# One decoder step on one core: a fixed order of products up to the MLP, more 48-product sequences, a second norm by fp32r products, and a shared last multiplication

## The chip, the cores and the metric

The kernel runs on 1 core of one Trainium2 chip. A core has a matrix engine (TensorE, in the profile PE for products and PEld for weight loads), three engines for elementwise work (VectorE or DVE, ScalarE or ACT, GpSimd or POOL), SyncE (SP) that issues transfers, and 16 DMA engines. The metric is the device time of one execution in microseconds (us). The kernel before has a median of 1088.29 us over three runs (1088.22 to 1089.59).

## The reference

One layer of a hybrid decoder is computed for 256 prompt positions and 8 x 4 sample positions, T = 288 columns in all, in float32:

```
h = rmsnorm(x, norm1_g);  proj = h @ w_in + b_in          # 2048 -> 3072
a, gate, z = proj split at 1024, 2048
u = a * sigmoid(gate)                                     # gated group
c = silu(layernorm(depthwise_conv31(history ++ u)))       # 1024 channels
d = windowed means of (history ++ z) - z                  # windows 2, 4, 8, 16, one per group of 256
p = (d_g @ pool_w[g] for 4 groups) * pool_scale           # 1024 channels
x = x + concat(c, p) @ w_out                              # 2048 -> 2048
h2 = rmsnorm(x, norm2_g)
x = x + square(relu(h2 @ w_ff1)) @ w_ff2                  # 2048 -> 8192 -> 2048
y = rmsnorm(x, norm_f)
```

The last 30 values of u and 15 of z are returned as new states. The columns of the norms are independent, so a row scale (1/rms) can be applied after a projection; the kernel does that.

## The kernel before

Channels lie on the 128 partitions, the 288 positions along the free axis, so x is 16 tiles of 128x288. Each float32 operand is split into a high part in fp32r (hi) and the remainder (lo), and a product is three fp32r products: hi x hi, hi x lo, lo x hi. `gemm` (line 291) issues them: two output tiles (m) at a time, input tiles (k) in pairs, six products per pair and m. An input tile's hi and lo lie in one four-row tile, and `classes` in `gemm` reorders the first products of a call by the row that they stream, as a string of 0 and 1 tells; `TURN` (line 70) is such a string for 48 products. It is used in four calls: c2, the third group of each half of w_out, and the third group of ff1.

Weights come from HBM in blocks of 8 input tiles, 256 columns wide (`load`, line 159), each in two halves of 128x1024; `split` (line 281) makes hi by ScalarE (L265) and lo by VectorE (V, L270), GpSimd (G, L273) or an accumulating DMA (D), as the table `WAYS` says for each stage. There are six buffers for raw halves and five for split ones. `ready` holds the weights made ahead for the next call; a call takes one entry and makes the next at its end.

The work goes through these stages, in the order of the program:
- a first pass over x with four output banks (c0 and c1 of the gated group) during the loads; the sum of squares for the first norm (`squares`, `first_sums`, `first_rows`) is reduced by small products on TensorE (L230), a root, and a spreading product (L250);
- `SEQUENCE` (line 45): c is a gated convolution pair (`conv_pair`: the 31 taps run as low-priority steps on VectorE, L434), p the projection of one pooling group (`pool_group`: GpSimd sums of line 466, VectorE's last split of d into `dx` at L478), P the pooling product `pool_products` that reads dx;
- w_out over the pooling half (`mixp`), with the products of the layernorm (`ln_mean`, `ln_sums`, `ln_rows`) in between, then over the convolution half (`mixc`);
- four rounds of ff1 (8 groups of 256 columns, 96 products each) and ff2. The second norm's sum of squares `ss2` is added up by GpSimd (L604); after the first ff1 group it goes through `rsqrt_rows` and scales each group's output;
- the last norm: small products, a root, spreading products, and a multiplication of the 16 tiles by VectorE in six pieces (L652), each followed by its store from SP's queue (L653).

A planner lays out each engine's instructions: by the rank in which the program traced them, among those whose inputs are ready in its own timeline. `later()` puts work at a low rank. `tc.issue_after(ins)` keeps what it covers behind `ins` on the same engine. In the kernel before, TensorE's order is therefore the planner's except in a few places; it put P1 into c7 and P0 into the first w_out group.

Of the kernel before, what the change touches and what calls it, by code (L numbers as in the profile page):

```python
# [16 lines left out]
P = 128  # L17
# [27 lines left out]
SEQUENCE = [(_s[0], int(_s[1])) for _s in "c0 c1 c2 c3 c4 p3 c5 p2 P3 c6 p1 P2 p0 P1 c7 P0".split()]  # L45
# [41 lines left out]
def trunk_kernel(ctx: ExitStack, tc: tile.TileContext, io):  # L87
# [133 lines left out]
    def rsqrt_sums(parts, scale, after=None, busy=(0, 0)):  # L221
# [5 lines left out]
        idle = cvp.tile([P, 512], F32, name=nm("idle"), tag="cv") if sum(busy) else None  # L227
        for n, t in enumerate(parts):
            for j in range(3):
                last = nc.tensor.matmul(pt[:TB, j : j + 1], t[:, j * TB : (j + 1) * TB], ones[:, 0:1], start=n + j == 0, stop=n == len(parts) - 1 and j == 2)  # L230
            with tc.issue_after(last.ins):
                for j in range(busy[n] if n < 2 else 0):
                    nc.tensor.matmul(idle[:, 0:P], ones, ones, start=True, stop=True)  # L233
# [12 lines left out]
    def spread(sums):  # L246

        s, pr, _ = sums
        for j in range(3):
            last = nc.tensor.matmul(pr[:, j * TB : (j + 1) * TB], s[:, j : j + 1].to_broadcast([TB, P]), ident, start=j == 0, stop=j == 2)  # L250
        return pr, last

    def rsqrt_rows(*args):
        return spread(rsqrt_sums(*args))[0]

# [34 lines left out]

    def gemm(banks, rhs, m_outer=False, between={}, classes=""):
# [3 lines left out]
        gets = ready.pop()  # L295
        step = 2 if len(banks) == 2 else 1
        pairs = [(k, m) for k in range(0, n, step) for m in range(len(banks))]
        if m_outer:
            pairs.sort(key=lambda km: km[1])
        if step == 2:  # L300
            parts = ((0, 0, 0), (1, 0, 0), (0, 1, 0), (1, 1, 0), (1, 0, 1), (0, 0, 1))
        else:
            parts = ((0, 0, 0), (0, 0, 1), (0, 1, 0))
        todo = [(k + d, m, w, x) for k, m in pairs for d, w, x in parts]
# [5 lines left out]
        ahead = None  # L310
        for j, (k, m, w, x) in enumerate(todo):
            if j % (len(banks) * len(parts)) == 0:
                ahead = between[k]() if k in between else None
            with tc.issue_after(ahead.ins) if ahead is not None else nullcontext():
                last = nc.tensor.matmul(banks[m][:, :T], gets[k // 8](k % 8, m)[w], rhs[k][x], start=j == ends[m][0], stop=j == ends[m][1])  # L315
# [167 lines left out]
    def pool_products(g):  # L483

        bk = ms("pp")
        gemm(each(bk), halves(dd[g]))
        for m, (mh, ml) in enumerate(halves(dd[g])):
# [3 lines left out]
            mixp[i] = (mh, ml)  # L491

# [15 lines left out]
    with tc.issue_after(gemm(pair0 + pair1, hx, between={15: first_sums})):  # L508
        third = conv_products(2, between={2: first_rows}, classes="01" * 18 + TURN)
# [3 lines left out]
    conv_pair(2, third)  # L513
    for kind, i in SEQUENCE[3:]:
        if kind == "c":
            conv_pair(i, conv_products(i))
        elif kind == "p":
            pool_group(i)
        else:
# [8 lines left out]
    def ln_mean():  # L528
        norm["mean"] = ms("pmean")[:, 0, :T]
        nc.tensor.matmul(norm["mean"], ones, sum_c[:, 0, :], start=True, stop=False)  # L530
        return nc.tensor.matmul(norm["mean"], ones, cs[-1][:, 1, :], start=False, stop=True)
# [20 lines left out]
    behind = nullcontext()  # L552
    for g in range(8):
        bk = bank2()
        with behind:
# [156 lines left out]
```

## Time and profile before

| | |
|---|---|
| median of 3 runs | 1088.29 us |
| profiled execution | 1087.97 us |
| its span, first to last instruction | 1086.2 us |
| mean granted TensorE clock | 0.997 |
| TensorE's products | 8206, busy 1073.7 us |
| VectorE / ScalarE / GpSimd busy | 634.0 / 477.9 / 182.7 us |
| read from HBM / written | 185.16 / 4.28 MB |

The profile shows one execution. A row of a timeline gives start, length, engine, line, operation, output and inputs, and how many instructions were merged, in brackets the idle time before and what ended it. A row of a stretch gives busy time and, in brackets, the instructions touched for each engine, then the granted clock, the share of the DMA engines and GB/s. Products are pipelined: one lasts some 0.29 us while the next starts after 0.13, so starts and not lengths show the pace.

### The profile page before, as it was taken

What the parts mean: (1) busy time and instruction counts of PE and PEld (TensorE: products, weight loads), DVE (VectorE), ACT (ScalarE), POOL (GpSimd) and SP (SyncE); (2) the same over time, 40 slices, a digit from 0 to 9 for tenths busy, and PEclk for the clock granted to TensorE, in tenths of its full rate; (3) what the DMA queues carried; (4) which work ended last, traced back from release to release, by engine and by line L of the source; (5) the groups of instructions that cost most, each with busy time, mean ns of one, the idle gap of its engine ahead of it and who ended that gap; (6) DMA issues with size and microseconds to landing.
All of it is one profiled execution on the core that took longest, in us unless ns stands there. A gap on an engine that the chain in (4) does not pass through costs nothing.

```text
span 1086.2 us, 19609 instructions
## 1 busy us (share of the span) xinstructions
PE 1073.7 (99%) x8206; PEld 1071.4 (99%) x8206; DVE 634.0 (58%) x813; ACT 477.9 (44%) x583; POOL 182.7 (17%) x212
## 2 busy tenths in 40 slices
PE   9999999999999999999999999999999999999996
PEld 8999999999999999999999999999999999999996
DVE  7899999678555444445454444545544445554553
ACT  8654445475544433334443333444433334444441
POOL 0888989613000000000000000000000000000000
PEclk9999999999999999999999999999999999999998
DMA  9896467545455555555555555555555555555522
GB/s 333 281 269 177 136 178 245 183 153 178 159 171 169 164 172 174 166 167 173 167 167 172 172 165 168 175 167 165 174 169 165 172 173 165 167 174 166 168 76 88
DMA packets 58120, 190.71 MB, mean 176 GB/s; under 512 B 6192, under 2 KB 11312, under 8 KB 58032
## 3 DMA queue, kind: packets, MB, share of 16 engines
q1 hardware_dynamic: 56480, 185.27, 52.2%
q0 software_dynamic: 1008, 3.67, 1.9%
q8 instruction: 64, 1.05, 0.4%
q10 hardware_dynamic: 544, 0.52, 0.1%
q14 instruction: 24, 0.20, 0.0%
HBM read 185.16 MB, written 4.28 MB: 174 GB/s over the span
## 4 chain that ended last, share of the span: by engine, by line
PE 96%; DVE 1%; ACT 1%; DMA 1%; issue 1%; POOL 0%; DVEq 0%
PE ac L315 95%; DMA wr<-in_w 1%; PE pp L315 0%; DVE xT L652 0%; ACT whi L265 0%; DVE wlo L270 0%; POOL wlo L273 0%; PE idle L233 0%; ACT n L567 0%; PE pt L250 0%; PE pt L230 0%; DVE z_all L391 0%; ACT z_all L389 0%; ACT hx L340 0%; DVE n L564 0%
## 5 line engine op out<-in xcount | busy, mean ns | idle before, releaser
L265 ACT CAST whi<-wr 128x1024 fp32r<-128x1024 f32 (+1 forms) x341 | 356.6, 1046 | 558.4 <-PE ac L315 540.4
L270 DVE TENSOR_TENSOR wlo<-wr,whi 128x1024 fp32r<-128x1024 f32 (+1 forms) x295 | 362.9, 1231 | 350.3 <-ACT whi L265 350.3
L315 PE MATMUL ac<-ax,whi 128*128 128x288 f32 x2048 | 351.5, 292 | 0.0
L315 PE MATMUL ac<-fx,whi 128*128 128x288 f32 x2048 | 350.1, 292 | 0.0
L315 PEld LDWEIGHTS ac<-ax,whi 128*128 128x128 f32 x2048 | 296.2, 187 | 0.0
L315 PEld LDWEIGHTS ac<-fx,whi 128*128 128x128 f32 x2048 | 295.6, 187 | 0.0
L315 PE MATMUL ac<-ax,wlo 128*128 128x288 f32 x1024 | 217.4, 292 | 0.0
L315 PE MATMUL ac<-fx,wlo 128*128 128x288 f32 x1024 | 216.3, 292 | 0.0
L315 PEld LDWEIGHTS ac<-ax,wlo 128*128 128x128 f32 x1024 | 162.7, 187 | 0.0
L315 PEld LDWEIGHTS ac<-fx,wlo 128*128 128x128 f32 x1024 | 162.2, 187 | 0.0
L315 PE MATMUL ac<-hx,whi 128*128 128x288 f32 x768 | 136.3, 295 | 0.6 <-DVE hx L338 0.6
L315 PEld LDWEIGHTS ac<-hx,whi 128*128 128x128 f32 x768 | 113.8, 188 | 1.0 <-ACT whi L265 0.8
L273 POOL TENSOR_TENSOR wlo<-wr,whi 128x512 fp32r<-128x512 f32 x78 | 105.9, 1411 | 32.7 <-ACT whi L265 30.4
L434 DVE SCALAR_TENSOR_TENSOR pc<-u_all,vec,pc 128x256 f32<-128x256 f32 x232 | 99.8, 483 | 3.0 <-ACT pc L431 1.6
L315 PE MATMUL ac<-hx,wlo 128*128 128x288 f32 x384 | 86.1, 296 | 0.3 <-DVE wlo L270 0.2
L315 PEld LDWEIGHTS ac<-hx,wlo 128*128 128x128 f32 x384 | 62.7, 188 | 1.1 <-DVE wlo L270 0.9
L315 PE MATMUL ac<-dx,whi 128*128 128x288 f32 x256 | 46.1, 296 | 0.0
L315 PE MATMUL ac<-mx,whi 128*128 128x288 f32 x256 | 45.2, 294 | 0.1
L617 DVE SCALAR_TENSOR_TENSOR t<-ac,r 128x576 f32<-128x576 f32 x32 | 24.2, 758 | 26.3 <-PE ac L315 25.2
L315 PEld LDWEIGHTS ac<-mx,whi 128*128 128x128 f32 x256 | 37.5, 188 | 0.6 <-ACT mx L569 0.3
L315 PEld LDWEIGHTS ac<-dx,whi 128*128 128x128 f32 x256 | 38.0, 188 | 0.1
L646 DVE TENSOR_TENSOR xT<-xT,ac 128x576 f32<-128x576 f32 x24 | 18.1, 754 | 19.4 <-PE ac L315 19.4
(108 smaller groups left out, 502.9 us busy)
## 6 DMA issues: line engine op xcount, KB each, us to landing
wr<-in_w SPq DMA_DIRECT2D x335, 512.0 KB, 3.6
wlo<-in_w POOLq DMA_DIRECT2D x7, 512.0 KB, 7.3
xT<-in_xT SPq DMA_DIRECT2D x7, 288.0 KB, 6.6
out_u_out<-u_all SPq DMA_DIRECT2D x1, 1208.0 KB, 9.7
out_yT<-xT SPq DMA_DIRECT2D x2, 576.0 KB, 2.9
u_all<-in_hist_c SPq DMA_DIRECT2D x8, 136.0 KB, 5.2
wr<-in_w SPq DMA_DIRECT2D x4, 256.0 KB, 3.3
out_z_out<-z_all SPq DMA_DIRECT2D x1, 668.0 KB, 8.2
```

The costliest lines, as they stand in the source:

```text
L265: nc.scalar.copy(hi, raw)
L270: nc.vector.tensor_tensor(lo, raw, f32(hi), op=ALU.subtract)
L273: nc.gpsimd.tensor_tensor(lo[:, j : j + 2, :], raw[:, j : j + 2, :], f32(hi[:, j : j + 2, :]), op=ALU.subtract)
L315: last = nc.tensor.matmul(banks[m][:, :T], gets[k // 8](k % 8, m)[w], rhs[k][x], start=j == ends[m][0], stop=j == ends[m][1])
L434: nc.vector.scalar_tensor_tensor(out=dst, in0=up[:, w : w + SEQ], scalar=cwv[:, w : w + 1], in1=pc, op0=ALU.mult, op1=ALU.add)
L617: nc.vector.scalar_tensor_tensor(out=t, in0=bk[:, :, :T], scalar=0.0, in1=both(r2), op0=ALU.max, op1=ALU.mult)
L646: nc.vector.tensor_tensor(x2, x2, bk[:, :, :T], op=ALU.add)
```

## The change

- Once the first pass is traced, every product through the third ff1 group is chained behind the one before it (`mm`, `chain`), so TensorE follows the program's order there.
- `gemm` takes input tiles in pairs for four banks too (after two single ones), and calls a hook in `between` without chaining to it separately. `ready` is a queue, first in, first out.
- `TURN` stands in eleven calls: the first pass's tail, c2, c4 to c7, the second and the fifth group of both halves of w_out, and the second ff1 group.
- The first norm's small products move from the first pass to the head of c2. P1 moves into c7, behind its first 48 products, and its weights behind c7's; from there on `ready` holds two entries.
- The second norm: ss2 is split into hi and lo and multiplied by a 128x128 matrix of 1/2048 in two fp32r products after 24 products of the first ff1 group; the root and its refinement then run over all 288 columns.
- The last norm takes the root straight from the summing products; VectorE multiplies tiles 0 to 11 from the spread row in PSUM, GpSimd tiles 12 to 15 from a copy, and the stores alternate between SP's and ScalarE's queues. Four small filler products follow the last sums in place of six.
- The norm gains are loaded ahead of the first tile of x.

```diff
-SEQUENCE = [... "c0 c1 c2 c3 c4 p3 c5 p2 P3 c6 p1 P2 p0 P1 c7 P0".split()]
+SEQUENCE = [... "c0 c1 c2 c3 c4 p3 c5 p2 P3 c6 p1 P2 p0 c7 P1 P0".split()]
+TURNS = ("c4", "c5", "c6", "c7")
...
+    nc.sync.dma_start(vec[:, 0:NG], io["vec"][:, 0:NG])
     for k, n in FIRST[:6]:
         first_x(k, n)
-        if k == 0:
-            nc.sync.dma_start(vec[:, 0:NG], io["vec"][:, 0:NG])
-        elif k > 1:
+        if k > 1:
             first_weights(k, n, nc.sync)
...
+    means = const.tile([P, P], F32R, name="means")
+    nc.vector.tensor_scalar(means, ones, DC / D, None, op0=ALU.mult)
...
+    def inverse_root(mean, root, y, out):
+        nc.vector.reciprocal(y, root)
+        nc.vector.scalar_tensor_tensor(out=root, in0=mean, scalar=EPS, in1=y, op0=ALU.add, op1=ALU.mult)
+        nc.vector.scalar_tensor_tensor(out=root, in0=root, scalar=-0.5, in1=y, op0=ALU.mult, op1=ALU.mult)
+        nc.vector.scalar_tensor_tensor(out=out, in0=root, scalar=1.5, in1=y, op0=ALU.add, op1=ALU.mult)
...
+    chain = []
+    def mm(*args, **kw):
+        with tc.issue_after(chain[-1]) if chain else nullcontext():
+            last = nc.tensor.matmul(*args, **kw)
+        if chain:
+            chain[0] = last.ins
+        return last
...
-        gets = ready.pop()
-        step = 2 if len(banks) == 2 else 1
-        pairs = [(k, m) for k in range(0, n, step) for m in range(len(banks))]
+        gets = ready.pop(0)
+        units = [(k, 2) for k in range(0, n, 2)]
+        if len(banks) == 4:
+            units[:1] = [(0, 1), (1, 1)]
+        pairs = [(k, width, m) for k, width in units for m in range(len(banks))]
...
+            if begins.get(j) in between:
+                between[begins[j]]()
+            last = mm(banks[m][:, :T], gets[k // 8](k % 8, m)[w], rhs[k][x], start=j == ends[m][0], stop=j == ends[m][1])
...
-    with tc.issue_after(gemm(pair0 + pair1, hx, between={15: first_sums})):
-        third = conv_products(2, between={2: first_rows}, classes="01" * 18 + TURN)
+    chain.append(gemm(pair0 + pair1, hx, classes="010" * 4 + "101" * 4 + "01" * 24 + TURN))
+    third = conv_products(2, between={0: first_sums, 4: first_rows}, classes="01" * 15 + TURN)
...
+    def pool_between():
+        ready.extend(itertools.islice(weights, 1))
+        return pool_products(1)
     for kind, i in SEQUENCE[3:]:
         if kind == "c":
-            conv_pair(i, conv_products(i))
+            conv_pair(i, conv_products(i, between={8: pool_between} if i == 7 else {}, classes=TURN if f"c{i}" in TURNS else ""))
         elif kind == "p":
             pool_group(i)
-        else:
+        elif i != 1:
             pool_products(i)
...
-            last = gemm(each(bk), [mixp[k] for k in korder], between=BETWEEN.get(g, {}), classes=TURN if g == 2 else "")
+        gemm(each(bk), [mixp[k] for k in korder], between=BETWEEN.get(g, {}), classes=TURN if g in (1, 4) else "")
...
-        gemm(each(bk), mixc, classes=TURN if g == 2 else "")
+        gemm(each(bk), mixc, classes=TURN if g in (1, 4) else "")
...
+    def second_rows():
+        hl = actp.tile([P, 4, T], F32R, name="hl", tag="act")
+        hi, lo = hl[:, 1, :], hl[:, 0, :]
+        nc.scalar.copy(hi, ss2)
+        nc.vector.tensor_tensor(lo, ss2, f32(hi), op=ALU.subtract)
+        bk, r2 = ms("mean2"), row("r2")
+        mean, root = bk[:, 0, :T], bk[:, 1, :T]
+        mm(mean, means, hi, start=True, stop=False)
+        last = mm(mean, means, lo, start=False, stop=True)
+        nc.scalar.activation(root, mean, AF.Sqrt, bias=eps)
+        inverse_root(mean, root, r2, r2)
...
-            gemm(each(bk), x1, classes=TURN if ch == 0 and g == 2 else "")
-            if ch == 0 and g == 0:
-                nc.scalar.copy(r2, rsqrt_rows([ss2], 1.0 / D))
+            gemm(each(bk), x1, between={4: second_rows} if ch == 0 and g == 0 else {}, classes=TURN if ch == 0 and g == 1 else "")
+            if ch == 0 and g == 2:
+                chain.clear()
...
-    rf = rsqrt_rows([ssf, qf], 1.0 / D, None, (3, 6))
-    for k0, n in ((0, 1), (1, 2), (3, 4), (7, 4), (11, 3), (14, 2)):
-        xk = xT[:, k0 : k0 + n, :]
-        nc.vector.tensor_tensor(xk, xk, rf[:, None, :T].to_broadcast([P, n, T]), op=ALU.mult)
-        nc.sync.dma_start(io["yT"][:, k0 : k0 + n, :], xk)
...
+    nc.scalar.activation(root, sums_f, AF.Sqrt, bias=eps[:TB, :])
+    inverse_root(sums_f, root, first, s_f)
...
+    queues = (nc.sync, nc.scalar)
+    def finish(eng, r, pieces):
+        for j, (k0, n) in enumerate(pieces):
+            xk = xT[:, k0 : k0 + n, :]
+            eng.tensor_tensor(xk, xk, r[:, None, :].to_broadcast([P, n, T]), op=ALU.mult)
+            queues[j % 2].dma_start(io["yT"][:, k0 : k0 + n, :], xk)
+    finish(nc.vector, rows_f, ((0, 1), (1, 1), (2, 2), (4, 2), (6, 3), (9, 3)))
+    nc.scalar.copy(rf, rows_f)
+    finish(nc.gpsimd, rf, [(k, 1) for k in range(12, KT)])
```

More of the change, by code (lines that the diff above doesn't have):

```diff
@@ L219, in trunk_kernel, with rsqrt_sums @@
     nc.gpsimd.memset(u_all[:, :, 0:CH], 0.0)
[L221 removed]
+    means = const.tile([P, P], F32R, name="means")
+    nc.vector.tensor_scalar(means, ones, DC / D, None, op0=ALU.mult)
+    cst = const.tile([P, 32], F32, name="cst")
+    eps, mean_d = cst[:, 0:1], cst[:, 1:2]
+    nc.vector.memset(eps, EPS)
+    nc.vector.memset(mean_d, 1.0 / D)
+    def inverse_root(mean, root, y, out):
[3 more added lines that the diff above has]
+        nc.vector.scalar_tensor_tensor(out=out, in0=root, scalar=1.5, in1=y, op0=ALU.add, op1=ALU.mult)
+    def rsqrt_sums(parts, scale, after=None):
         pq = ms("pt")
         pt = pq[:, 0, :]
[L227 removed]
         for n, t in enumerate(parts):
             for j in range(3):
[L230 to L233, printed above, removed]
+                last = mm(pt[:TB, j : j + 1], t[:, j * TB : (j + 1) * TB], ones[:, 0:1], start=n + j == 0, stop=n == len(parts) - 1 and j == 2)
         st = const.tile([TB, 12], F32, name=nm("st"))
```

55 lines of the change are left out of this document (32 added, 23 removed).

## The prediction

> **What bounds the kernel now.** I read the page's busy times and its chain first, then TensorE's instructions in order of time, then the stages where a wait of TensorE ends.
>
> ```profile
> PE 1073.7 (99%) x8206; PEld 1071.4 (99%) x8206; DVE 634.0 (58%) x813; ACT 477.9 (44%) x583; POOL 182.7 (17%) x212
> PE 96%; DVE 1%; ACT 1%; DMA 1%; issue 1%; POOL 0%; DVEq 0%
> ```
>
> TensorE is the chain. Of its 8206 products 8112 are the projections' (line 315: 1152 for w_in, 48 pooling, 768 for w_out, 6144 in the MLP), so what counts is how closely they follow one another. The next rows are TensorE's instructions by start time (start, length, group, count), then two stretches with the products touched in brackets.
>
> ```profile
> 84.57 0.70 PE L315 MATMUL ac<-hx,whi 128*128 128x288 f32 x4
> ...
> 87.77 0.43 PE L315 MATMUL ac<-hx,whi 128*128 128x288 f32 x2
> 180.58:187.16 6.58, 6.58 (x53) 6.58 (x51) 5.77 (x12) 2.32 (x3) 6.58 (x7) 1.00 0.76 251
> 187.16:193.40 6.24, 6.24 (x51) 6.24 (x49) 5.07 (x11) 2.10 (x3) 6.24 (x7) 1.00 0.58 180
> 77.00:165.60 88.60, 88.60 (x665) 88.47 (x665) 86.43 (x174) 42.42 (x63) 81.18 (x84) 1.00 0.61 175
> 165.60:180.20 14.60, 14.53 (x110) 14.29 (x108) 14.25 (x31) 9.14 (x13) 14.60 (x15) 1.00 0.81 236
> ```
>
> From 84.57 to 87.77 there are four groups of six: 24 products in 3.20 us, 133.3 ns each. From 187.16 to 193.40 there are 48 (three more overlap the edges): 130.0 ns each. The form is the same, nothing idles and the granted clock is 1.00 in both, so the stream has two rhythms. The stretch from 180.58 holds the 48-product sequence `TURN` of the third w_out group: 50 products in 6.58 us, 131.6 ns. Before it the rhythm is slow, after it fast. The slow one began at a stumble:
>
> ```profile
> 77.21 0.68 PE L315 MATMUL ac<-hx,whi 128*128 128x288 f32 x4
> 77.80 0.54 PE L315 MATMUL ac<-hx,wlo 128*128 128x288 f32 x2
> ```
>
> Four products at 130 ns should end the first row at 77.73; the lo part came 0.07 late and the slow rhythm lasted until the next `TURN`, 102 us on. DVE (86.4 of 88.6 us) and POOL (81.2) are nearly full there as well: this stage has two more engines close behind TensorE.
>
> **The change part by part.** The sum is made against the profiled execution, 1087.97 us (span 1086.2 and 1.8 around it); the median of the three runs is 0.3 above.
>
> *Rhythm.* Between 77.8 and 180.2 run 665 + 110 products less the edges, about 765; at 3.33 ns each 2.5 us is lost. A `TURN` in c4, c5, c6, c7 and in the second and fifth groups of both halves of w_out should keep this fast. The late lo part at 77.80 stays (its load is not changed), so 48 products of p3 stay slow, 0.16. One w_out group and one ff1 group sooner, and a turn already at the end of the first pass, give some 0.4 more. Eleven sequences in place of four cost up to 7 x 48 x 1.6 ns = 0.54; how dear one is that starts in the fast rhythm no row shows, so I take half, 0.3. Net -2.5 + 0.16 - 0.4 + 0.3 = -2.4; ends: 0 (no hold) and -3.0 (turns cost nothing, all hold, p3 too).
>
> [...]
>
> *Fixed order.* Now every product waits for the one before it in program order; what is late stops all of TensorE, and no later product fills in. Three places are tight. First P1 and P0, the pooling products, which read dx (rows of the chain and of three engines in order of time):
>
> ```profile
> 137.00 1.60 PE pp L315 x12
> 138.60 20.75 PE ac L315 x156
> 138.22 2.56 POOL L273 TENSOR_TENSOR wlo<-wr,whi 128x512 fp32r<-128x512 f32 x2 [2.55 <-ACT whi L265]
> 145.34 5.05 POOL L273 TENSOR_TENSOR wlo<-wr,whi 128x512 fp32r<-128x512 f32 x4
> 159.44 0.75 DVE L478 TENSOR_TENSOR dx<-d,dx 128x576 fp32r<-128x576 f32 x1
> 160.97 0.42 PE L315 MATMUL pp<-dx,whi 128*128 128x288 f32 x2
> 167.73 1.67 DVE L478 TENSOR_TENSOR dx<-d,dx 128x576 fp32r<-128x576 f32 x1
> 169.65 0.43 PE L315 MATMUL pp<-dx,whi 128*128 128x288 f32 x2
> ```
>
> p1 ends at 137.00 and its dx is whole at 160.19: 23.2 us. In the new order P1 comes after P2 (1.6), p0 (96 products) and 48 of c7, 18.8: 20.4 us, 2.8 too early. p0 ends at 138.60 + 96 x 0.1333 = 151.4 and its dx is whole at 169.40: 18.0. The new order leaves c7 and P1, 108 products, 14.1 us, and the 2.8: another 1.1 of waiting. Upper end +3.9. Lower end: no wait. Much of the two chains is queueing (5.05 us of other splits at 145.34 while chain 1 is unfinished), POOL sat idle 2.55 us just ahead at 138.22, and P1's weights no longer take a split buffer ahead of c7's, so POOL can begin c7's sooner. The row with the idle time is nearest to what moves; it covers most of 2.8, and what is left of 3.9 is about 1.3. A TensorE that runs 2.5 us ahead also frees buffers sooner, which I put at 1.0. I take +0.3.
>
> Second, the sum of squares at the head of c2: its last sum ended at 29.4 (27.94 + 1.43) and the six products that read it ran at 30.98; they now come at c2's head, not sooner, so 1.6 us are free, about one split. Taken 0, end +0.5. While TensorE waits there, nothing else is queued on it that could run.
>
> ```profile
> 27.94 1.43 DVE L393 TENSOR_TENSOR z_all<-z_all 128x288 f32<-128x288 f32 x1
> 30.98 0.43 PE pt L230 x6
> 32.81 1.22 DVE L242 SCALAR_TENSOR_TENSOR st<-st 96x3 f32<-96x3 f32 x1
> 34.07 0.16 DVE L243 SCALAR_TENSOR_TENSOR st<-st 96x3 f32<-96x3 f32 x1
> ```
>
> *Second norm.* Twelve small products leave, two fp32r products (0.26) come, 24 products into ff1:
>
> ```profile
> 271.48 0.42 PE L315 MATMUL ac<-ax,whi 128*128 128x288 f32 x2
> 273.64 2.00 POOL L604 TENSOR_TENSOR ss<-ss,q 128x288 f32<-128x288 f32 x2 [4.23 <-ACT q L603]
> 274.80 1.06 ACT L265 CAST whi<-wr 128x1024 fp32r<-128x1024 f32 x1 [0.53 <-PE ac L315]
> 283.96 0.59 PE L230 MATMUL pt<-ones,ss 128*96 128x1 f32 x6
> 284.41 0.51 PE L315 MATMUL ac<-ax,whi 128*128 128x288 f32 x2
> 290.07 0.80 PE L250 MATMUL pt<-ident,st 96*128 96x96 f32 x6
> 290.66 0.51 PE L315 MATMUL ac<-ax,whi 128*128 128x288 f32 x2
> L615 ACT COPY r<-pt 128x288 f32<-128x288 f32 x1 | 0.4, 400 | 1.9 <-PE pt L250 1.9
> 1071.98 0.45 DVE L635 TENSOR_TENSOR xT<-xT,ac 128x288 f32<-128x288 f32 x1 [4.81 <-PE ac L315]
> ```
>
> Leaving: 0.45 + 0.59 and a late restart after each, 1.1. Coming: 24 products after 271.48 is 274.60, but ss2 is whole at 275.64. ACT's copy to hi (0.40, perhaps behind the split that ends at 275.86) gives 276.1 to 276.3, DVE's subtraction (0.45, as the 288-column one at 1071.98) 276.6 to 276.8: TensorE stands 2.0 to 2.2 and pays 0.26. Net +1.2; ends +0.8 and, with one of DVE's splits (1.2) in front, +2.4. What follows (root, four DVE steps over 288 columns, some 3.5 us) must end before the third ff1 group, over 20 us on: covered.
>
> *Tail.* The root is taken straight from the sums (one DVE step gone), DVE multiplies 12 tiles, POOL 4, two queues send.
>
> ```profile
> 1073.67 0.16 DVE L236 TENSOR_SCALAR st<-pt 96x3 f32<-96x3 f32 x1 [1.24 <-PE pt L230]
> 1073.86 0.21 ACT L237 ACTIVATE st<-st 96x3 f32<-96x3 f32 x1 [0.38 <-DVE st L236]
> 1075.85 5.28 DVE L652 TENSOR_TENSOR xT<-xT,pt 128x288 f32<-128x288 f32 x6 [1.00 <-PE pt L250]
> 1077.00:1078.00 1.00, 0.00 (x0) 0.00 (x0) 1.00 (x1) 0.00 (x0) 0.00 (x0) 1.00 0.57 207
> 1078.00:1079.00 1.00, 0.00 (x0) 0.00 (x0) 1.00 (x2) 0.00 (x0) 0.00 (x0) 1.00 0.62 235
> 1080.00:1081.00 1.00, 0.00 (x0) 0.00 (x0) 1.00 (x2) 0.00 (x0) 0.00 (x0) 0.50 1.03 410
> L443 POOL TENSOR_TENSOR sum_c<-c,c 128x288 f32<-128x288 f32 x2 | 1.6, 806 | 0.0
> ```
>
> The step is worth 0.19. DVE's 12 tiles take 12/16 of 5.28, 4.0; POOL's four 0.4 + 4 x 0.81 = 3.6: production ends 1.3 sooner. But the DMA share is 1.03 at 1080, and only the first two rows leave room, (410 - 207 + 410 - 235)/410 = 0.9 us. So -0.19 - 0.9 = -1.1; ends -0.2 (no fill) and -1.9.
>
> POOL can hold DVE up: the three-element step at 32.81 took 1.22, beside POOL's split, where its like took 0.16. [...]
>
> *Hidden.* The norm gains (vec) go first on SP's queue, ahead of xT's first tile, which comes one issue later; the first DVE step waited for vec:
>
> ```profile
> 5.12 0.37 DVE L338 TENSOR_SCALAR hx<-xT,vec 128x288 fp32r<-128x288 f32 x1 [4.14 <-DMA vec<-in_vec]
> ```
>
> I take -0.1, ends -0.4 and +0.4 (xT then late). The first pass in pairs: two k's weights are already loaded and split as one piece: 0 within 0.3. From c7 on weights are split one group further ahead; there are five buffers and ACT (44%) waits for them to come free, so nothing changes; with that cover gone, one more split (1.05) would stand ahead of each group's evacuation.
>
> **Sum.** 1087.97 - 2.4 (rhythm) + 0.3 (P1, P0) + 1.2 (second norm) - 1.1 (tail) - 0.1 (start) = 1085.9. All the good ends together give 1087.97 - 3.0 + 0.0 + 0.8 - 1.9 - 0.4 = 1083.5; without the wait in the second norm, whose rows I trust most, 1082.5.
>
> **Rivals.**
> - *TensorE waits at P1 and P0 as long as the rows say* (+3.9 for 0.3): 1089.5. For it: both chains took 23 and 18 us. Against: POOL's idle time ahead. Chance 0.24, no measurable change.
> - *The turns do not hold up to w_out*: a turn met in the fast rhythm may end it. All four of now began in the slow one; seven new ones may not. 1085.9 + 2.4 = 1088.3, chance 0.06. [...] DVE locked out in the tail: POOL's 3.2 on top of DVE's 4.0 in place of 5.28, so +1.9 for -1.1, 1088.9, chance 0.02.
> - *Slower: the last turn fails.* It stands in ff1's second group and sets the rhythm of the rest: 6144 - 192 products x 3.33 ns = 19.8 us, 1105.6. It decides if the stream behind that group shows 133 ns. For: the two late fp32r products precede it by only 72 products. Against: 4 of 4 turns ended fast. Chance 0.07.
> - *Slower by waits at many groups*: in the fixed order each late split stops TensorE in the stage where POOL is full; from 5 us beyond my sum it is slower, 1091 to 1094. Chance 0.13.
>
> **How the numbers follow.** A measurement of this kernel tells 0.2%, 2.2 us (1086.1 to 1090.5). My forecast's own range is 1082.5 to 1086.1, chance 0.48; within 0.2%: 0.24 + 0.06 + 0.02 = 0.32; slower: 0.07 + 0.13 = 0.20. The range reaches from there through the first rival, 1082.5 to 1090.5.
>
> **What will show it.** Right: windows of 48 products from c4 on last 6.24 us, not 6.40; TensorE stands about 2 us some 24 products into ff1; the DMA share in the tail is near 1 from its second us. P1's and P0's first products follow without a gap. Wrong: 133 ns behind any turn, gaps over 1 us in front of the pooling products, or a gap at c2's head.

## The result, and the profile after

The changed kernel takes 1100.29 us (median of 4 runs, 1100.06 to 1101.24) where the kernel before takes 1088.26 (1087.8 to 1089.59): a ratio of 1.011, with a 95% interval from 1.0093 to 1.0128. It is 12.0 us slower; 1085.9 was predicted, in a range up to 1090.5.

The profiled execution has a span of 1098.4 us against 1086.2, 12.2 more. The busy times and the chain on its page:

```profile
PE 1076.7 (98%) x8192; PEld 1072.3 (98%) x8192; DVE 633.8 (58%) x815; ACT 476.9 (43%) x584; POOL 184.7 (17%) x216
...
PE 69%; issue 21%; POOL 4%; DVE 4%; DMA 1%; ACT 1%; SPq 0%; POOLq 0%; DVEq 0%; ACTq 0%
```

TensorE was 96% of the chain before; now GpSimd and VectorE have 4% each, so something of theirs is waited for ("issue" is time in which the engine waited for nothing that the profile shows). Which, says the view of TensorE's waits (engine and line, waited for what: us in total, times, longest). First the kernel before, then the changed one:

```profile
...
PE ac L315 <- DVE hx L338: 0.6, 1, 0.6
PE ac L315 <- DVE wlo L270: 0.2, 1, 0.2
```

```profile
PE pp L303 <- ACT dx L495: 2.4, 1, 2.4
PE pp L303 <- DVE dx L496: 1.5, 1, 1.5
PE mean L303 <- ACT hl L635: 1.5, 1, 1.5
...
PE ac L303 <- ACT mx L591: 1.0, 2, 0.6
PE mean L303 <- DVE hl L636: 0.9, 1, 0.9
...
PE ac L303 <- DVE mx L592: 0.6, 1, 0.6
...
```

Before, TensorE waited for next to nothing behind the start. Now it waits for `dx` (P1's operands), `hl` (the second norm's) and `mx` (what the layernorm gives), 7.9 us in six rows. To see the loss in full I numbered the 8112 products by their start and took, for each stretch, the time beyond 130.0 ns a product:

| stretch of products | before, us over | after | difference |
|---|---|---|---|
| start of the first product | 5.64 | 5.54 | -0.10 |
| 0 to 288: first pass, c2 | 3.19 | 4.55 | +1.36 |
| 288 to 1104: c3 to p0, c7 | 2.08 | 0.33 | -1.75 |
| 1104 to 1440: c7, P1, P0, w_out | 1.00 | 7.03 | +6.03 |
| 1440 to 1584: w_out, layernorm | 2.86 | 2.79 | -0.07 |
| 1584 to 1728: first groups behind the layernorm | 0.86 | 3.21 | +2.35 |
| 1728 to 1968 | 0.00 | 0.09 | +0.09 |
| 1968 to 2208: second norm | 1.58 | 4.99 | +3.41 |
| 2208 to 8111: the rest of the MLP | 0.00 | 0.00 | 0.00 |
| last product's start to the end of the span | 14.55 | 15.46 | +0.91 |

The sum is 12.2. At the two dearest places TensorE does not only stand. Chosen instructions in order of time at P1 and at the second norm (start, length, what, idle time ahead and its releaser):

```profile
156.96 0.29 PE L303 MATMUL ac<-hx,whi 128*128 128x288 f32 x1
158.91 0.67 ACT L495 CAST dx<-d 128x576 fp32r<-128x576 f32 x1 [0.44 <-POOL d L493]
159.64 0.53 PE L303 MATMUL pp<-dx,whi 128*128 128x288 f32 x2 [2.38 <-ACT dx L495]
160.54 1.42 DVE L496 TENSOR_TENSOR dx<-d,dx 128x576 fp32r<-128x576 f32 x1
162.02 1.33 PE L303 MATMUL pp<-dx,whi 128*128 128x288 f32 x4 [1.53 <-DVE dx L496]
...
282.70 1.04 ACT L272 CAST whi<-wr 128x1024 fp32r<-128x1024 f32 x1 [0.54 <-PE ac L303]
283.65 0.43 ACT L635 CAST hl<-ss 128x288 fp32r<-128x288 f32 x1
283.78 1.22 DVE L277 TENSOR_TENSOR wlo<-wr,whi 128x1024 fp32r<-128x1024 f32 x1
284.13 0.40 PE L303 MATMUL mean<-hl,means 128*128 128x288 f32 x1 [1.47 <-ACT hl L635]
284.92 0.45 DVE L636 TENSOR_TENSOR hl<-ss,hl 128x288 fp32r<-128x288 f32 x1
285.43 0.40 PE L303 MATMUL mean<-hl,means 128*128 128x288 f32 x1 [0.90 <-DVE hl L636]
```

and the same places by stretches (busy time and products of each engine, then the granted clock, the DMA share and GB/s):

```profile
156.00:160.00 4.00, 1.62 (x12) 1.38 (x11) 4.00 (x10) 1.72 (x2) 4.00 (x7) 1.00 1.06 179
160.00:162.00 2.00, 0.49 (x4) 0.20 (x2) 2.00 (x4) 0.00 (x0) 1.35 (x2) 0.56 1.07 162
162.00:163.00 1.00, 0.98 (x4) 0.98 (x5) 1.00 (x3) 0.00 (x0) 0.27 (x1) 0.50 1.10 119
166.00:167.00 1.00, 1.00 (x6) 1.00 (x6) 1.00 (x3) 0.76 (x2) 1.00 (x1) 0.50 0.98 401
286.40:288.00 1.60, 1.60 (x9) 1.60 (x8) 1.60 (x1) 0.00 (x0) 0.00 (x0) 0.54 0.80 294
```

From start to start the gap at P1 is 2.68 us and, four products on, 1.88; the clock then stands at 0.50, and until 167.2 the products follow one another at 240 ns. At the second norm the gaps are 1.76 and 1.30, and 14 products at 240 ns follow. Standing and running slowly have separate prices, and the experiments take them apart.

### The profile page after: what moved, and what is told of

Its sections match the earlier page's. It is cut to its first block, busy times and chain, and to the rows that moved or that the text cites. A ratio compares the mean times of both kernels' runs of the same rounds, so it can differ in the third digit from the quotient of the medians.

```text
span 1098.4 us, 19596 instructions
## 1 busy us (share of the span) xinstructions
PE 1076.7 (98%) x8192; PEld 1072.3 (98%) x8192; DVE 633.8 (58%) x815; ACT 476.9 (43%) x584; POOL 184.7 (17%) x216
## 4 chain that ended last, share of the span: by engine, by line
PE 69%; issue 21%; POOL 4%; DVE 4%; DMA 1%; ACT 1%; SPq 0%; POOLq 0%; DVEq 0%; ACTq 0%
PE ac L303 69%; POOL wlo L280 2%; DVE pc L452 2%; POOL s L484 1%; DMA wr<-in_w 1%; DVE wlo L277 1%; PE pp L303 0%; POOL prd L456 0%; ACT whi L272 0%; DVE dx L496 0%; POOL xT L708 0%; ACT n L589 0%; PE pt L303 0%; DVE z_all L409 0%; ACT z_all L407 0%
## 5 line engine op out<-in xcount | busy, mean ns | idle before, releaser
L303 PE MATMUL ac<-hx,whi 128*128 128x288 f32 x768 | 139.1, 296 | 0.5 <-DVE hx L356 0.3
L708 POOL TENSOR_TENSOR xT<-xT,rf 128x288 f32<-128x288 f32 x4 | 3.0, 789 | 808.5 <-ACT rf L712 808.5
L280 POOL TENSOR_TENSOR wlo<-wr,whi 128x512 fp32r<-128x512 f32 x78 | 108.3, 1415 | 36.2 <-ACT whi L272 35.3
```

The lines of the kernel that those rows point to most:

```text
L280: nc.gpsimd.tensor_tensor(lo[:, j : j + 2, :], raw[:, j : j + 2, :], f32(hi[:, j : j + 2, :]), op=ALU.subtract)
L303: last = nc.tensor.matmul(*args, **kw)
L708: eng.tensor_tensor(xk, xk, r[:, None, :].to_broadcast([P, n, T]), op=ALU.mult)
```

## The experiments

All but one start from the changed kernel; ratios are to the kernel before, run on the same chip in the same hours.

**1. No order at all.** The chain is never begun.

```
-    chain.append(gemm(pair0 + pair1, hx, classes=...))
+    gemm(pair0 + pair1, hx, classes=...)
```

> Edit: the changed kernel without the chain of products (each product is free of the one before it; turns, second norm, tail and sequence stay). Theory T (the loss is TensorE standing in the fixed order at three places: P1 inside c7 +6.2 us, the first product group after the layernorm +2.4, the second norm's two products +3.4): most of these 12.0 go, and of the 2.2 us that the fast rhythm brought a part goes as well, since no order holds the turns: 1088.3 to 1090.5. Rival R1 (the loss comes from the other edits: splits made one group further ahead, the norm gains first on the queue, eleven turns): 1097 to 1101.

Measured: 1099.32 us, ratio 1.0102 (1.0082 to 1.0121). The number is the rival's, the reason is not: TensorE waits elsewhere, 2.4 us at P0 and 3.8 us for `mx` at 225.9. The kernel before was never without order; it had c2 behind the first pass, products behind small products, w_out's last groups in sequence. This edit takes that away too, so it tells nothing about the fixed order against the old one. Experiment 8 does.

**2. The waits filled.** 18 idle products ahead of P1's, 13 ahead of the second norm's.

```
         bk = ms("pp")
+        fill(bk, 18 if g == 1 else 0)   # mm(bk[:, 1, 288:416], ones, ones, start=True, stop=True)
...
+        fill(bk, 13)
         mm(mean, means, hi, start=True, stop=False)
```

> Edit: the chain stays; 18 idle products of 128 fp32 columns (0.21 us each) stand ahead of P1's first product and 13 ahead of the second norm's, in the time in which TensorE stood still. Theory T2 (behind a wait of some 4 and 3 us the products run at 240 ns because TensorE had stood: the clock was lowered): no product at 240 ns behind either place, 2.1 + 1.5 = 3.6 us less, 1096.7, the waits themselves as long as before. Rival R2 (240 ns from the operands or the banks read there): the same products at 240 ns, 1100.3 or slightly more.

Measured: 1097.22, ratio 1.0078 (1.0061 to 1.0094): 3.1 us less for work that gives nothing. The stretches of this run at P1:

```profile
156.00:160.00 4.00, 4.00 (x37) 4.00 (x36) 4.00 (x11) 1.72 (x2) 4.00 (x8) 1.00 1.11 189
164.00:168.00 4.00, 4.00 (x32) 4.00 (x31) 4.00 (x10) 3.30 (x5) 1.97 (x2) 1.00 0.82 315
```

The clock stays at 1.00, and no run of products at 240 ns is left behind either place; P1's stretch (products 1104 to 1200) costs 2.1 us less, the second norm's 1.5, as expected. The mean granted clock tells the same of the runs without a trace: 0.995 or 0.996 in all four, where the changed kernel has 0.991 in all four. The half rate came from standing, not from the operands, which are the same here.

**3. The last copy ahead of the stores.**

```
+    nc.scalar.copy(rf, rows_f)
     finish(nc.vector, rows_f, ((0, 1), (1, 1), (2, 2), (4, 2), (6, 3), (9, 3)))
-    nc.scalar.copy(rf, rows_f)
     finish(nc.gpsimd, rf, [(k, 1) for k in range(12, KT)])
```

> Edit: ScalarE's copy of the last scale (the one that POOL's four multiplications read) is queued ahead of the three stores on the same queue. Theory T3 (copy at 1091.6, 4.1 us after VectorE's first multiplication, only since three stores that wait for VectorE stand ahead of it): copy 0.1 us after the first multiplication starts, POOL done near 1091.2, last store's issue no later than 1092, DMA share near 1 until some 1095, end 2.0 to 2.5 us sooner: 1098.0. Rival R3 (the DMA engines set the end, or POOL and VectorE hold each other up): under 0.7 us, 1099.6 or more.

Measured: 1098.09, ratio 1.0087 (1.0072 to 1.0102), 2.2 us less. The tail of the changed kernel in order of time, then this run's, and one of its stretches:

```profile
1087.10 4.08 DVE L708 TENSOR_TENSOR xT<-xT,ends 128x288 f32<-128x288 f32 x6 [1.00 <-PE ends L700]
1087.58 7.13 SPq L709 DMA_DIRECT2D out_yT<-xT  x5
1087.95 3.60 ACTq L709 DMA_DIRECT2D out_yT<-xT  x3
1091.59 0.40 ACT L712 COPY rf<-ends 128x288 f32<-128x288 f32 x1 [6.34 <-DVE xT L708]
1092.06 3.03 POOL L708 TENSOR_TENSOR xT<-xT,rf 128x288 f32<-128x288 f32 x4 [808.54 <-ACT rf L712]
```

```profile
1086.80 0.40 ACT L711 COPY rf<-ends 128x288 f32<-128x288 f32 x1 [1.85 <-PE ends L700]
1087.23 4.08 DVE L708 TENSOR_TENSOR xT<-xT,ends 128x288 f32<-128x288 f32 x6 [1.43 <-ACT rf L711]
1087.28 3.06 POOL L708 TENSOR_TENSOR xT<-xT,rf 128x288 f32<-128x288 f32 x4 [803.85 <-ACT rf L711]
```

```profile
1092.00:1093.00 1.00, 0.00 (x0) 0.00 (x0) 0.00 (x0) 0.00 (x0) 0.00 (x0) 0.50 1.04 414
```

In the changed kernel ScalarE could not copy before 1091.59, since its queue held three stores that wait for VectorE's products; so GpSimd began when VectorE had ended. With the copy first both multiply at once, and neither is slower for it (4.08 and 3.06 us, 4.08 and 3.03 one after the other). From there the DMA engines set the end: their share is 1.04 to 1.09 from 1089 to 1094.

**4. Turns in the old places only.**

```
-TURNS = ("c4", "c5", "c6", "c7")
+TURNS = ()
...
-classes=TURN if g in (1, 4) else ""
+classes=TURN if g == 2 else ""        # both halves of w_out; in the MLP g == 1 becomes g == 2
```

> Edit: the 48-product sequences only in the four places where the kernel before had them (third group of c's, third group of both halves of w_out, third of the first product of the MLP); the chain and all else stay. Theory T4 (the added sequences keep the rhythm of 130 ns where 133 ns was): 1.7 to 2.2 us slower, 1102.3, windows of 48 products at 6.40 us between c2 and w_out's third group. Rival R4 (the rhythm comes from the fixed order alone): 1100.3, 6.24 us. Second rival (seven more sequences cost 0.05 to 0.09 each and hold nothing): 1099.8.

Measured: 1100.43, ratio 1.0111 (1.0096 to 1.0126): the first rival. Between products 288 and 1104 this run is 0.00 us over 130 ns a product, the changed kernel 0.33. Two stretches of 48 products:

```profile
99.00:105.24 6.24, 6.24 (x50) 6.24 (x49) 6.00 (x16) 2.61 (x3) 5.90 (x9) 1.00 0.50 168
125.00:131.24 6.24, 6.24 (x50) 6.24 (x49) 5.20 (x10) 3.60 (x5) 6.07 (x10) 1.00 0.50 170
```

The fast rhythm needs no turn here; the four added turns of this stretch cost 0.33. When a turn is needed, experiment 11 shows.

**5. Both late places later.**

```
-between={8: pool_between} ... between={4: second_rows}
+between={14: pool_between} ... between={12: second_rows}
```

> Edit: P1's products stand 36 products later in c7 (ahead of its last 12) and the second norm's two products 48 later in the MLP's first group (72 products in). The first is 4.7 us, the second 6.2 us later; P1's operands were whole at 162.0, P1 would come at 161.6 without its wait, and the second norm's at 284.9, its products would come at 288.6. Theory T (the wait is as long as the operands are late at that place): P1 waits under 0.5 us, the second norm not at all, both stretches at 240 ns go (2.1 + 1.5), P0 may now wait up to 3 us (its operands at 167.8): 1091 to 1094. Rival (the operands are late because TensorE itself is: they come later by as much): 1099 to 1101.

Measured: 1098.24, ratio 1.0081 (1.0064 to 1.0098). The second norm is as expected: no wait, its stretch 0.35 us over in place of 4.99. P1 waits for nothing, but P0, 12 products of c7 behind it, waits 6.5 us, and 24 products at 240 ns follow. VectorE releases it, in this order:

```profile
169.58 1.43 DVE L496 TENSOR_TENSOR dx<-d,dx 128x576 fp32r<-128x576 f32 x1
171.68 0.51 DVE L509 SCALAR_TENSOR_TENSOR dx<-pp,vec,dx 128x288 fp32r<-128x288 f32 x1
172.25 0.85 PE L303 MATMUL pp<-dx,whi 128*128 128x288 f32 x2 [6.47 <-DVE dx L509]
```

P0's own operand (L496) is whole at 171.0, 3.3 us later than in the changed kernel (167.75), and most of the wait is for that; what it waits for last, 1.2 us more, is L509, which empties P1's sums out of `pp`, of which there is one buffer. So neither side had all of it: P1 placed close ahead of P0 makes a new wait, and VectorE, which is busy for all 12.00 us from 160 to 172, is what both waits are for.

**6. The first two groups behind the layernorm free.**

```
+        if g == 0:
+            chain.clear()
-        gemm(each(bk), mixc, classes=...)
+        last = gemm(each(bk), mixc, classes=...)
+        if g == 1:
+            chain.append(last)
```

> Edit: the products of the first two groups behind the layernorm are not chained (a product of the second group may go ahead of one whose operand is late); the chain holds before and behind them. Theory T (the 2.35 us lost there are lost to the fixed order): 1098.0, no more gaps behind 226 than the kernel before shows. Rival (the layernorm's results come later in themselves): under 0.7 us gained, 1099.6 or more.

Measured: 1097.46, ratio 1.0077 (1.0059 to 1.0095). The stretch 1584 to 1728 falls from 3.21 to 1.03 us over, as theory T has it. The profiled execution, at 1096.11 the fastest of the four, shows one thing more. The second norm's gaps are the same as in the changed kernel, 1.76 and 1.30, but the stretch around them costs 1.5 us less (3.47 over in place of 4.99), since the clock did not fall. Why, the clock shows: in each trace it changes only at times a whole number of 3.41 us apart (in the changed kernel at 160.22, 167.05, 286.52 and 289.93), and the marks lie elsewhere in each trace. The next rows cut the time at the marks, first in the changed kernel, then in this run:

```profile
279.69:283.10 3.41, 2.98 (x23) 2.75 (x22) 3.08 (x4) 2.87 (x6) 1.48 (x2) 1.00 0.56 167
283.10:286.52 3.42, 1.49 (x9) 1.28 (x10) 2.42 (x4) 2.74 (x4) 0.42 (x1) 1.00 0.55 159
286.52:289.93 3.41, 3.41 (x16) 3.41 (x16) 3.21 (x4) 0.00 (x0) 0.00 (x0) 0.50 0.37 135
```

```profile
277.48:280.89 3.41, 2.49 (x20) 2.25 (x18) 3.08 (x4) 2.87 (x6) 1.90 (x2) 1.00 0.58 162
280.89:284.31 3.42, 1.98 (x13) 1.77 (x14) 2.42 (x4) 2.25 (x4) 0.00 (x0) 1.00 0.49 177
284.31:287.72 3.41, 3.41 (x28) 3.41 (x27) 2.99 (x5) 1.05 (x1) 0.00 (x0) 1.00 0.27 100
```

In the changed kernel one window of 3.41 us holds most of both waits, 1.93 us of idle TensorE, and the next window runs at 0.50; here a mark divides them, 0.92 and 1.44 us to a window, and nothing happens. The other three runs have a mean clock of 0.990 to 0.992 against 0.995 here, so part of this run's lead over the median is likely that chance.

**7. Splits one group ahead again.**

```
-        ready.extend(itertools.islice(weights, 1))
+        if more:                               # more=False for c7
+            ready.extend(itertools.islice(weights, 1))
```

> Edit: c7 no longer calls for the next group's weights, so that from c7 on splits are made one group ahead, as in the kernel before; all else stays. Theory D (splits of the group after next stand ahead of the pooling steps, the layernorm's and the second norm's small steps on ScalarE, VectorE and GpSimd; with the chain gone 5 to 8 us were still lost): P1's wait shorter by 1 to 3 us, the second norm's gaps shorter by 1 to 2 us, the layernorm's by up to 2: 1094 to 1097. Rival (five split buffers bound how far ahead the splits get, so depth does nothing): within 1 us of 1100.3.

Measured: 1100.23, ratio 1.0103 (1.0088 to 1.0118), with the same waits (2.4, 1.4, 1.5, 0.9): the rival. The depth of the splits does nothing.

**8. The old order with the rest of the change.** The chain goes; `issue_after` stands where the kernel before has it.

```
-    chain.append(gemm(pair0 + pair1, hx, classes=...))
-    third = conv_products(2, ...)
+    first = (gemm(pair0 + pair1, hx, classes=...))
+    with tc.issue_after(first):
+        third = conv_products(2, ...)
...
+            with tc.issue_after(ahead.ins) if ahead is not None else nullcontext():   # products behind small products
...
+        behind = tc.issue_after(last) if g > 3 else nullcontext()                     # w_out's last groups
```

> Edit: the chain is replaced by the order that the kernel before has (c2 behind the first pass, a group's products behind the small products put between them, w_out's last groups behind one another), with everything else of the change kept. Theory T (the fixed order is what costs): 1088 to 1092. Rival D (depth of the splits and P1's new place cost, order or not): 1095 to 1099. With all products free of any order it had been 1099.3, where the layernorm alone stood still for 4.1 us at 225.9; that gap should be gone here, since w_out's last groups are in order again.

Measured: 1091.96, ratio 1.0022 (1.0011 to 1.0033): 8.3 us less than with the fixed order (9.6 by the two ratios). Behind the layernorm it is 0.86 us over, as before, at the second norm 0.59, less than before. In the profiled run, the slowest of the ten, one wait of some size is left behind the start, again P0's, and the clock falls behind it. P0's operand (L498) is whole at 172.02, 2.6 us later than before (169.40), and the emptying of `pp` (L511) ends 1.2 us behind that:

```profile
PE pp L303 <- DVE dx L511: 2.5, 1, 2.5
```

```profile
170.50 1.52 DVE L498 TENSOR_TENSOR dx<-d,dx 128x576 fp32r<-128x576 f32 x1
...
172.70 0.51 DVE L511 SCALAR_TENSOR_TENSOR dx<-pp,vec,dx 128x288 fp32r<-128x288 f32 x1
```

```profile
173.00:174.50 1.50, 1.24 (x5) 1.25 (x6) 1.50 (x5) 1.48 (x2) 0.71 (x2) 0.54 0.26 104
174.50:176.00 1.50, 1.50 (x8) 1.50 (x7) 0.66 (x3) 1.32 (x3) 1.50 (x2) 0.50 0.40 144
```

**9. The norm gains behind xT's first tile again.**

```
-    nc.sync.dma_start(vec[:, 0:NG], io["vec"][:, 0:NG])
     for k, n in FIRST[:6]:
         first_x(k, n)
+        if k == 0:
+            nc.sync.dma_start(vec[:, 0:NG], io["vec"][:, 0:NG])
```

> Edit: the norm gains are again issued behind xT's first tile, as in the kernel before; all else of the change stays. In the profiles so far the first 96 products of the changed kernel and its variants took 2.4 to 4.9 us more than 96 x 130 ns, 1.6 in the one profile of the kernel before. Theory S (the gains ahead of xT make the later weight loads land later): 0.8 to 1.3 us less, 1099.2, first 96 products within 0.4 of the kernel before. Rival (loads land as chance has it, or the pairs of the first pass cost it): within 0.5 of 1100.3, 2.4 or more over in the first 96 products.

Measured: 1100.98, ratio 1.0119 (1.0105 to 1.0133), the first 96 products 2.98 us over: not the gains.

**10. The old first pass**, one k at a time, in the changed kernel, and order and place of P1 apart.

```
-        units = [(k, 2) for k in range(0, n, 2)]
-        if len(banks) == 4:
-            units[:1] = [(0, 1), (1, 1)]
+        step = 2 if len(banks) == 2 else 1
+        units = [(k, step) for k in range(0, n, step)]
```

> Edit: the changed kernel with the old first pass (one k at a time, no sequence set); chain, places, second norm, tail stay. Theory F: 1098.5 to 1099.3, first 96 products at 1.6 over. Rival L: 1099.8 to 1100.8; the load of the third and fourth weights lands at 8.1 to 10.4 in the profile, and the first 96 products are late by as much.

Measured: 1099.9, ratio 1.0097 (1.0074 to 1.0121), first 96 products 2.20 over: rival L. Over all 17 profiles of this study the cast of the third and fourth weights, which waits for their load, begins between 8.14 and 10.41 us: at 8.14, 8.32, 8.62 and 9.64 with the old first pass, at 8.36 to 10.41 with the new. Where the load's issue was read it was at 2.58 in both. The product with number 96 starts between 19.7 and 22.4. A loss of the first pass in pairs is not shown, nor excluded to some tenths.

P1 ahead of c7 again, with the old order (as in experiment 8) and with the chain:

```
-... "P2 p0 c7 P1 P0"
+... "P2 p0 P1 c7 P0"
```

> Edit: the changed kernel with the order of the kernel before and, besides, P1 ahead of c7 again (splits one group ahead with it). With the old order alone 1092.0 was measured; there TensorE stood 2.7 us at P0 and ran half as fast for 14 products behind it. Theory P (P1's new place inside c7 makes P0's operands late): that gap goes, 1087.5 to 1088.5. Rival (VectorE's and GpSimd's queues are late there whatever P1's place): gap at P0 or at w_out as before, 1091 to 1092.5.

> Edit: the changed kernel, chain and all, with P1 ahead of c7 again. Its operands were whole at 160.2 to 162.0 in every profile, its place comes at about 151. Theory T (a chained product waits until its operand is whole, wherever it stands): TensorE stands for 8 to 10 us ahead of P1 and runs at half the clock behind it, P0 does not wait: 1102 to 1106. Rival (the planner brings the operands of P1 forward when its place comes sooner): under 5 us, 1098 to 1101.

Measured: 1089.04 with the old order, ratio 1.0004 (0.9994 to 1.0013), between the two expectations: the wait at P0 is gone, as theory P has it, and a gap of 1.3 us for a `wlo` of GpSimd's stands at 164.9. So 11.3 of the 12.0 us go with the old order and the old place. With the chain it is 1103.0 (a single run). There TensorE stands, as theory T says:

```profile
157.44 0.85 PE L303 MATMUL pp<-dx,whi 128*128 128x288 f32 x2 [7.17 <-ACT dx L495]
```

| | P1 inside c7 | P1 ahead of c7 |
|---|---|---|
| fixed order | 1100.29 | 1103.0 |
| old order | 1091.96 | 1089.04 |

The new place is a help under the fixed order (2.7, against one run) and a loss without it (2.9), by P0's later operand and the wait for `pp`; the fixed order costs 8.3 and 14.0. The cells come from different chips: by the ratios to the kernel before the loss is 2.0, and the intervals of the two just touch (1.0011 to 1.0033 and 0.9994 to 1.0013).

**11. The chain only where nothing was late**, from the first pass to p0, once on the kernel before and twice on the changed one; there the order, P1's place and the turns are again those of the kernel before, and the gains stand behind xT's first tile.

```
+            if i == 1:
+                chain.clear()            # ahead of P1
             pool_products(i)
```

> Edit, on the kernel before: its products behind the first pass are chained in program order up to the end of p0, nothing else. Theory T (the order alone keeps 130 ns, no turn needed, and up to p0 no operand is late): 2.1 us less, 1086.1, windows of 48 products at 6.24 us from c3 to p0. Rival 1 (operands are late up to p0 as well without the new first pass): gaps there, 1088 or more. Rival 2 (gained in front, waited for at P0 or the layernorm): rhythm as in T, total within 0.7 of the kernel before.

> Edit: the products are chained only from the first pass to the end of p0, where no operand was late (first 288 to 1104 products: 2.08 us over 130 ns each before, 0.00 in the chain without added turns); from P1 on the order, the place of P1 and the turns of the kernel before; gains behind xT's first tile; second norm 72 products into the MLP; last copy ahead of the stores. Theory T: 1088.2 - 2.1 (rhythm) - 1.2 (second norm: 0.35 over in place of 1.58) - 0.9 (tail: end 13.6 behind the last product's start in place of 14.55) = 1084.0, between 1083 and 1086. Rival (GpSimd and VectorE are the bound of the first stage: what TensorE gains there it waits for at P0 or the layernorm): 1086 to 1089.

> Edit, on the version chained from the first pass to p0 (1086.5): the first pass again one k at a time in the old order, without a sequence set. Theory F (the first pass in pairs costs 0.8 to 3.3 us at its loads): 1084.5 to 1085.7, first 96 products at 1.6 over 96 x 130 ns, first pair's products by 9.5 us. Rival L (the loads of the third and fourth weights land between 8.1 and 10.4 us as chance has it): 1086.0 to 1087.0.

On the kernel before: 1089.09, ratio 1.0005 (0.9996 to 1.0014), no gain, the number of rival 1. In the profiled run, the slowest of its eleven, a split's lo part comes late by DMA and nothing may go ahead of it:

```profile
PE ac L226 <- DMA wlo<-in_w: 1.9, 1, 1.9
```

```profile
66.00:69.00 3.00, 3.00 (x14) 3.00 (x14) 2.78 (x4) 0.00 (x0) 0.31 (x1) 0.50 1.02 352
```

The gap of 2.14 us, the half clock behind it and then the slow rhythm make this stretch 5.92 us over (2.08 before), as rival 1 has it. Whether this load was late by chance is not shown: the eleven runs go from 1087.53 to 1092.13, and one was traced.

With the changed kernel's second norm (late) and tail (copy first): 1086.54, ratio 0.9978 (0.9968 to 0.9988), and with the old first pass 1086.6, ratio 0.998 (0.9966 to 0.9993). Both beat the kernel before by 0.2%, 1.7 us, less than the 4.2 expected, and the number lies in the rival's range: in the first's profile, its slowest run, the first 96 products are 2.57 over those of before, by a late load of weights (cast at 10.41), and a gap of 1.5 us stands at 165.8, for a `wlo`. The stretch 288 to 1104 is 0.00 in the first and 1.93 in the second, with no turn there in either. In the second, one product that reads `wlo` took 159 ns at 79.17 and the rhythm changed:

```profile
60.00:66.24 6.24, 6.24 (x50) 6.24 (x49) 5.85 (x16) 3.67 (x4) 6.12 (x8) 1.00 1.04 274
99.00:105.40 6.40, 6.40 (x50) 6.40 (x49) 6.16 (x16) 2.20 (x3) 6.07 (x8) 1.00 0.46 158
```

So a stumble of 29 ns was enough to start the slow rhythm; not every stop does (behind P1's stop of some 3 us in experiment 4 the products run at 130.0), and in no trace did it end but at a turn. Where nothing stumbles, a turn is worth nothing; where something does, it is worth what it cuts off: in experiment 8 a product came 0.11 us late at 80.53, c5's turn ended the slow rhythm, and the stretch 288 to 1104 is 0.59 us over, where the kernel before, with the same stumble at 77.80 and no turn there, has 2.08.

## Why the prediction was wrong, by its own steps

*P1 and P0: +0.3, upper end +3.9; it was +6.0.* This is the step that failed. It let GpSimd's idle 2.55 us and a TensorE that runs ahead absorb most of the wait. Neither did: GpSimd's idle time there shrank to 1.43 us and `dx` came later all the same. TensorE was hardly ahead: p1's products ended 0.1 us sooner than before (136.88), since the first pass had lost 1.3. And VectorE began to empty their sums a microsecond later than before:

```profile
138.93 0.74 DVE L475 TENSOR_TENSOR tz<-ac,rb 128x576 f32<-128x576 f32 x1
...
134.00:158.00 24.00, 23.26 (x179) 23.02 (x177) 24.00 (x50) 11.69 (x20) 21.73 (x21) 1.00 0.47 151
```

It began at 137.91 before. It is busy for all 24.00 us of that stretch, GpSimd for 21.7 (before, 24.00 and 21.45: as full), and `dx` was whole at 161.96 against 160.19. Of these 1.8 us, 1.2 were lost when ScalarE's copy began (158.91 against 157.71); the rest is VectorE's subtraction, 1.42 us in place of 0.75. The small steps behind p1 wait in two full queues and did not follow TensorE; what put them later than before no run isolates, and experiment 7 shows that it was not the depth of the splits. Even the upper end was low, because the price of a wait was taken to be the wait: about 4.3 us of standing, all of it at P1 (2.68 + 1.88 less two products), where 3.9 were reckoned for P1 and P0, and 2.1 for the lowered clock, which the sum did not have.

*Three tight places.* There were four. The first group behind the layernorm (+2.35) was not on the list. Before, later products went ahead of those whose `mx` was late, and the trace showed no gap; the sign to look for was not a gap but products out of their program order (their `whi` and `wlo` come irregularly there; of which group they are, the views do not tell). Experiment 6 shows this term by itself.

*Second norm: +1.2, upper end +2.4; it was +3.4.* Without the clock it would be +1.9 (3.47 over in experiments 2 and 6), between the value taken and the upper end, for the reason given there, a split in front, but on both engines: ACT's cast to hi stands behind the split at 282.70, DVE's subtraction behind the one at 283.78. The clock is 1.5 on top. The fp32r products themselves are no loss: in the old order the stretch is 0.59 over against 1.58, though part of that is the sooner turn.

*Rhythm: -2.4; it was -1.97* (-1.75, and -0.22 behind P0). Right in size, not in cause, so this was luck: the same came without the added turns. The reading that a turn ends the slow rhythm holds; that it was needed did not, and each cost some 0.08 (0.33 for four), the full price and not half.

*Tail: -1.1, ends -0.2 and -1.9; it was +0.9.* The step followed what each engine computes and not each engine's queue: the copy stands behind three stores on ACT's queue. With it moved, the end is 0.9 sooner than before (13.6 us behind the last product's start against 14.55). That GpSimd would not hold VectorE up in the tail, as it seemed to in the step of 1.22 us at 32.81, was an estimate; here it was right: VectorE's twelve tiles, multiplied from PSUM, took 4.08 us beside GpSimd (experiment 3) and 4.08 us before it.

*Start: -0.1; the first product was 0.10 sooner.* The first pass (0 within 0.3) was +1.3 in this profile, within what the loads vary (the first 96 products are 1.59 to 4.89 over in the 17 profiles). *Squares at c2's head: 0* and *splits further ahead: 0* were right (c2's stretch +0.05; experiment 7).

The rival "slower by waits at many groups" had the sign, with 0.13 and 1091 to 1094; its cause, late splits all along the stage, did not come. Three small places did most of it, two of them with the clock. The last turn did not fail: the MLP runs at 130 ns. Of the marks that were to show a wrong forecast, "gaps over 1 us in front of the pooling products" is the one that stood in the trace. One sum does not come out: without the wait in the second norm the good ends give 1081.8 (1083.5 less 0.8 and 0.84), not 1082.5.

## What to carry to other kernels

Before the order of a bounding engine's work is fixed, list every operand that its queue would meet late, by the products that the trace shows out of program order and not only by its gaps; each becomes a stall, and in a stage where the other engines are full it does not shrink when the bounding engine runs ahead. Price a stall of some 2 us or more on TensorE, or several close together, at more than its length (1.5 to 2.1 us more in the changed kernel; nothing more for the second norm's pair in experiment 6, which a mark divided), and where it can't be moved, fill it. Where an engine both computes and issues stores, read its queue in order: a small step behind a store waits for whatever the store waits for (a copy at 1091.59 behind three stores, at 1086.80 ahead of them).

## What the runs showed of the hardware that was not expected

TensorE's granted clock fell to 0.50 after waits much shorter than I had thought to ask about, and products then started 240 ns apart for 2.4 to 5.8 us (10 to 24 products). Single waits of 2.02 (at the start of experiment 8), 2.14, 2.70 and 2.75 us had this after them, those of 1.3 to 1.6 no more than three such products. One of 2.79, at the start of the first of experiment 11's two versions of the changed kernel, had only two such products, and the second norm's pair of 1.76 and 1.30 had 10 to 15 in six kernels and at most one in two (experiment 6 and the chain with P1 ahead of c7): the length alone does not decide it.

What fits is the idle time within one window of the marks of experiment 6. Over all 17 traces, from the first products to the last of the MLP, each of the 18 windows at full clock with 1.86 us or more of idle TensorE was followed by one at 0.50, none with 1.44 or less was, and of three with 1.61 to 1.68 two were; the wait of 2.79 was divided by a mark, with 1.68 and 1.02 us idle on its two sides. In these traces the border lay between 1.44 and 1.86 us of idle time in a window of 3.41, and since the marks lie elsewhere in each trace, the same pair of waits cost 1.5 us more in the changed kernel than in experiment 6 (its stretch 4.99 us over against 3.47).

Products of one form had two rhythms, 130.0 and 133.3 ns, and which one ran depended on what went before: one product late by 29 ns (experiment 11, at 79.17) was enough to leave the fast one for some 600 products.
